# All gated rows of a mixer by seven block products, with ScalarE's deferrable work in a list of tasks

## The chip, the core and the metric

The kernel runs on one core of a Trainium2 chip. The metric is the device time of one execution in microseconds (us); the time before is the median of three runs. The engines named below are TensorE (PE in the profile; PEld is its weight load), VectorE (DVE), ScalarE (ACT), GpSimd (POOL) and SyncE (SP), which issues most of the loads.

## The reference

One step of an encoder trunk with two layers, for 640 tokens (512 of a prompt and 8 x 16 of running streams) with 1024 features, all in float32. Each layer is a feed-forward half-step, a mixer, and another feed-forward half-step. The change is in the mixer:

```
z = h @ w_in                      # conv B | conv C | conv V | q | k | v | gates
g_conv, g_attn = split(sigmoid(z_gates + b_gate))       # 1024 features each
y_conv = B * causal_conv3(C * V)                        # 512 features
y_attn = chunk-band attention, 8 heads of 64            # 512 features
m = g_conv * (y_conv @ w_conv_out) + g_attn * (y_attn @ w_attn_out)
x = x + m @ w_o
```

## The kernel before

**Numbers in two parts.** A float32 product is computed as three products of a faster 32-bit format: each operand is split into a high half (a cast on ScalarE) and a low half (source minus high half, on VectorE), and TensorE does hi x hi, hi x lo and lo x hi. So every weight needs one cast and one subtraction before it can be used.

**Weights.** The weights come as slabs of 128 x 1024, in the order of use, through three buffers (`raw`); their halves stand in three buffers each (`whi`, `wlo`). `prep` (line 351) casts the next slab on ScalarE and notes its low half; `flush` (line 367) issues the noted subtractions on VectorE; `source` (line 302) loads a slab and makes the sums of weight blocks. `slab` takes the next slab and prepares the one three places on; `quiet` only takes it; `ahead` makes the next slab's sums early.

**Seven products for eight.** Where two output rows of 128 features (or a row's two halves of the inner dimension) and two halves of the 640 tokens form a 2 x 2 block problem, the kernel uses the Winograd form of Strassen's scheme: seven block products instead of eight, with sums of weight blocks, sums of operand blocks ("mixing"), and sums of results. The seven are called by their operands: 11, 21, N6, T5, T7, 22, T4. Operands N6, T5, T7 and T4 are mixed, the other three are parts of the operand itself. A block product is 12 matmuls of 128 x 128 by 320 columns here. Such a group takes four weight slabs, the first three for two products each and the last for one. Each of seven products takes sums of weight blocks made on VectorE (one of them, in groups late enough, is summed by an accumulating DMA on GpSimd's queue, `lend_one`).

**The output stage** (`outputs`, line 1497) comes last in a mixer. It computes 16 gate rows of 128 features (0 to 7 for the conv branch, 8 to 15 for the attention branch) in pairs by `gate_pair` (the first pair is done earlier), and 8 output rows of each branch, which are multiplied by their gates and added up into `mm`. In it the instructions of TensorE, VectorE and ScalarE keep the order in which the program issues them, so each of these engines works through its own list, and an instruction that waits holds up all those behind it on its engine.

- `gate_pair(m)`: the products in the order 11, 21, N6, T5, T7, 22, T4. Product 11 goes into an accumulator `pa`; ScalarE copies it out (`c1`, capsm in the profile); then N6 adds to the same accumulator and is copied out (`u2`), and T7 and T4 add to it too. T5 goes into `pc`, is copied out (`c5`), and 22 adds to it. VectorE forms the rows u and g from these. u needs one more product with `rr` at the end, and a sigmoid on ScalarE comes after.
- `out(m)`: one row of a branch as a plain product over four blocks of the inner dimension, followed by the gating on VectorE.
- `rows`: four rows of a branch as one group of seven products, each into two 320-column parts, with the gating in between.

Before, rows 0 to 3 of each branch are plain (`out`), and rows 4 to 7 are a `rows` group. A sigmoid of u and g is kept in `lates` and issued by `due()` behind the copy of the next group's first product. The mixed operands of the conv branch are made step by step (`mixed`) between the plain rows and pair 4, those of the attention branch between pairs 8 and 14.

**Order of work before:** pair 2, four conv rows, pairs 4 and 6, conv rows 4 to 7, pair 8, two attention rows, pair 10, two attention rows, pairs 12 and 14, attention rows 4 to 7, and then the eight rows of the product with w_o.

Of the kernel before, what the change touches and what calls it, by code (L numbers as in the profile page):

```python
# [114 lines left out]
def mixer_order():  # L115

    mix = lambda *rows: ("mix", rows)
    out = [("v", None)] + [mix(("q", p), ("k", p)) for p in range(AW // P)]  # L120
    for c in range(0, CT, 2):
        out += [mix(("C", c + i), ("V", c + i)) for i in range(2)] + [mix(("B", c), ("B", c + 1))]
    gates = [mix(("g", m), ("g", m + 1)) for m in range(0, 2 * KT, 2)]
    out += gates[:2] + [("co", m) for m in range(4)] + gates[2:4] + [("rows", ("co", (4, 5, 6, 7)))]
    for i in range(2):
        out += [gates[4 + i], ("ao", 2 * i), ("ao", 2 * i + 1)]
    out += gates[6:] + [("rows", ("ao", (4, 5, 6, 7)))]
    return out + [("o", m) for m in range(KT)]
# [68 lines left out]
def trunk(ctx: ExitStack, tc: tile.TileContext, xin, wst, small, pbias, samplebias, kcache, vcache, gfin,  # L197
# [153 lines left out]
    def prep(i):  # L351
# [8 lines left out]
        o = 0  # L360
        for src, c in parts:
            d = slice(o, o + c.stop - c.start)
            o = d.stop
            ACT.copy(hi[:, d], src[:, c])  # L364
            pending.append((lo[:, d], src[:, c], hi[:, d]))

    def flush():
        for lo, src, hi in pending:
            DVE.tensor_tensor(out=lo, in0=src, in1=hi.bitcast(F32), op=ALU.subtract)  # L369
        pending.clear()  # L370
# [3 lines left out]
    def slab(hold=False):  # L374
# [10 lines left out]
        return ready[i], slabs[i]  # L385

# [1110 lines left out]
    def outputs(l, gp, X, st, cs, ycp, yas, sigmoid, gates):  # L1497
# [4 lines left out]
        ycs = [z[:, i] for z in ycp for i in range(2)]  # L1502
        mm = [spare[i // 2][:, i % 2] for i in range(CT)] + ycs
# [7 lines left out]
        lates = []  # L1511

        def due():
            for f in lates:
                f()
            lates.clear()

        def gate_pair(m, at):
            n = f"{l}_{m}"
            pa, pb, pc = (att(f"q{i}{n}")[:, :HT] for i in "abc")  # L1520
            s0 = quiet()
            block(pa, s0, 0, X11, every, True, True)
            ACT.copy(c1, pa)
            due()
            u, g = gates[m], gates[m + 1] = tmp(f"g{n}"), tmp(f"g{n}_1")
# [10 lines left out]
            ACT.copy(c5, pc)  # L1536
            at[1]()
            s2 = slab(True)[0]
# [5 lines left out]
            at[2]()  # L1544
            block(pc, s2, 1, X22, every, False, True)
            add(u[:, t2], pc, u2)
            s3 = slab(True)[0]
            DVE.tensor_tensor(out=u, in0=u, in1=rr, op=ALU.mult)
            lates.append(lambda: sigmoid(u, m))
            if m == 2:  # L1550
                for i in range(2):
                    sigmoid(gates[i], i)
            block(pa, s3, 0, XT4, every, False, True)
            DVE.tensor_tensor(out=g[:, t1], in0=pa, in1=rr[:, t1], op=ALU.mult)
            lates.append(lambda: sigmoid(g, m + 1, -1.0))
            flush()

        def parts(pool, tag, name, src):
            hi, lo = (pool.tile([P, T], F32R, tag=f"{tag}{i}", name=f"{name}{i}") for i in ("hi", "lo"))
            split(hi, lo, src)  # L1560
            return hi, lo

        def out(m, y, then=None, post=None):

            due()
            py = acc(f"py{l}_{m}")
            product(py, y)
            if then:
                then()
            g = gates[m]  # L1570
            if m < KT:
                DVE.tensor_tensor(out=halves(mm[m]), in0=two(py), in1=halves(g), op=ALU.mult)
            else:
                DVE.tensor_tensor(out=halves(g), in0=two(py), in1=halves(g), op=ALU.mult)
                add(mm[m - KT], mm[m - KT], g)
            flush()
            if post:
                post()

        yc, ya = [], []  # L1580
        mo = [None] * KT
        srcs = [yas[:, c, :] for c in range(CT)]
        x, moves = {}, []

        def take(y, name, cs, srcs):
            for c in cs:
                y.append(parts(gp, f"y{c}", f"{name}{l}_{c}", srcs[c]))

        def take_even(c):
            y = tuple(gp.tile([P, T], F32R, tag=f"y{c}{i}", name=f"ya{l}_{c}{i}") for i in ("hi", "lo"))  # L1590
            split(*(z[:, t1] for z in y), srcs[c][:, t1])
            ya.append(y)

        def low(lo, z, hi):
            DVE.tensor_tensor(out=lo, in0=z, in1=hi.bitcast(F32), op=ALU.subtract)

        def room(name):
            for k in EXTRA:
                x[name, k] = tuple(gp.tile([P, 2, HT], F32R, tag=f"x{EXTRA.index(k)}{i}",
                                           name=f"x{i}{name}{l}_{EXTRA.index(k)}") for i in ("hi", "lo"))  # L1600

        def minus(out, a):
            DVE.scalar_tensor_tensor(out=out, in0=a, scalar=-1.0, in1=out, op0=ALU.mult, op1=ALU.subtract)

        def mixed(i):

            z = ycp[i].rearrange("p c (a b) -> p (c a) b", a=2)
            e1, e2, o1, o2 = (z[:, k] for k in range(4))
            add(e1, e1, e2, ALU.subtract)
            add(e2, o2, e2, ALU.subtract)  # L1610
            minus(o2, e1)
            minus(o1, o2)
            yield
            for k in EXTRA:
                ACT.copy(x["co", k][0][:, i], z[:, 1 + EXTRA.index(k)])
            yield
            for k in EXTRA:
                hi, lo = (u[:, i] for u in x["co", k])
                low(lo, z[:, 1 + EXTRA.index(k)], hi)
            yield  # L1620
            hi, lo = (u[:, t2] for u in yc[2 * i])
            ACT.copy(hi, e1)
            yield
            low(lo, e1, hi)
            yield

        za = yas.rearrange("p (i c) (a b) -> p i (c a) b", i=2, a=2)

        def mix(n):

            e1, e2, o1, o2 = (za[:, :, k] for k in range(4))
            if n == 0:
                add(e1, e1, e2, ALU.subtract)
            elif n == 1:
                add(e2, o2, e2, ALU.subtract)
            else:
                minus(*((o2, e1) if n == 2 else (o1, o2)))

        def place(k):
            if k == XT5:  # L1640
                return [(*(u[:, t2] for u in ya[2 * i]), za[:, i, 0]) for i in range(2)]
            return [(*x["ao", k], za[:, :, 1 + EXTRA.index(k)])]

        def high(*ks):
            for k in ks:
                for hi, _, z in place(k):
                    ACT.copy(hi, z)

        def rest(*ks):
            for k in ks:  # L1650
                for hi, lo, z in place(k):
                    low(lo, z, hi)

        EXTRA = XT7, XT4, XN6

        def kind(name, i, k):
            if k in EXTRA:
                return tuple(z[:, i] for z in x[name, k])
            hi, lo = (yc if name == "co" else ya)[2 * i + (k in (X21, X22))]
            return tuple(z[:, t2 if k in (X22, XT5) else t1] for z in (hi, lo))  # L1660

        def rows(name, ms, first, mid=None, late=None, end=False, defer=False):

            n = f"{name}{l}_{ms[0]}"
            gs = [gates[m + (KT if name == "ao" else 0)] for m in ms]
# [3 lines left out]
            s1, s2, s5 = stage  # L1669

            def mul(ps, s, half, k, start):
                for u in range(2):
                    for i in range(2):
                        kp = half * NP + 2 * u + i
                        wh, wl = (z[:, kp * P : (kp + 1) * P] for z in s)
                        xh, xl = kind(name, i, k)
# [13 lines left out]
            def moved(r):  # L1690
                for u in range(2):
                    ACT.copy(mm[ms[2 * r + u]], gs[2 * r + u])

            w = quiet()
            mul(a, w, 0, X11, True)
            ACT.copy(s1, two(A))
            due()
            prep(used[0] + 1)
            flush()
            if first:  # L1700
                first()
            mul(b, w, 1, X21, True)
            add(s1, two(B), s1)
            w = slab(True)[0]
            flush()
            mul(a, w, 0, XN6, False)
            ACT.copy(s2, two(A))
            gated(0, [s1[:, u] for u in range(2)], t1)
            if mid:
                mid()  # L1710
            mul(c, w, 1, XT5, True)
            for u in range(2):
                ACT.copy(s5[:, u], c[u])
            w = slab(True)[0]
            mul(a, w, 0, XT7, False)
# [3 lines left out]
            if defer:  # L1719
                moves.append(lambda: gated(1, [s5[:, u] for u in range(2)], t2, -1.0))  # L1720
            else:
                gated(1, [s5[:, u] for u in range(2)], t2, -1.0)
            if late:
                late()
# [6 lines left out]
            if not end:  # L1731
                flush()
# [4 lines left out]
            if end:  # L1737
                flush()
# [700 lines left out]
```

## Time and profile before

| what | value |
|---|---|
| median of 3 runs | 2482.29 us (2481.04 to 2482.38) |
| span of the profiled execution, the time that the profile gives of it | 2479.9 us |
| median less that span | 2.4 us |
| granted TensorE clock, mean | 1.000 |
| TensorE busy | 2466.4 us, 99% |
| VectorE busy | 2182.6 us, 88% |
| ScalarE busy | 1386.7 us, 56% |
| output stage of layer 0 in the trace | from about 635 to 774 us |
| output stage of layer 1 in the trace | from about 1864 to 2003 us |

The span is counted from the first to the last instruction. A row of the timeline gives the start and the duration in us, the engine, the line of the kernel, the operation, output and inputs by their names in the program, and in brackets how long the engine was idle before and what ended that. A row of a grouped view gives the count, the busy time in us, the mean duration in ns, and the idle time before. A matmul's duration overlaps with the next one's, so TensorE's pace is read from the distance of the starts.

### The profile page before, as it was taken

How to read it: one execution, taken by the hardware profiler on the slowest of the kernel's cores; microseconds unless marked ns; L12 is line 12 of the kernel's file. 1: busy time of each engine (PE TensorE's matmuls, PEld its weight loads, DVE VectorE, ACT ScalarE, POOL GpSimd, SP SyncE). 2: the span in 40 equal slices, each digit the busy share in tenths (PEclk: the TensorE clock that was granted, in tenths of full speed). 3: DMA queues.
4: the chain of work that ended last, by engine and by line, in shares of the span. 5: the costliest groups of instructions: out<-in, count | busy, mean ns of one | idle time of the engine just before them, and what ended most of it. 6: DMA issues, size and time to landing. Idle time of an engine off the chain costs nothing.

```text
span 2479.9 us, 44056 instructions
## 1 busy us (share of the span) xinstructions
PE 2466.4 (99%) x17264; PEld 2414.6 (97%) x17264; DVE 2182.6 (88%) x3644; ACT 1386.7 (56%) x2231; POOL 320.8 (13%) x483
## 2 busy tenths in 40 slices
PE   9999999999999999999999999999999999999999
PEld 8999999889999999999999999998899999999998
DVE  7999998888888899998799999988888889999997
ACT  6555555665555555555665555566655556555555
POOL 0211112211000001111001010121110000111111
PEclk9999999999999999999999999999999999999999
DMA  4443444335344234444334343452453432444444
GB/s 155 128 120 101 124 117 120 114 110 175 102 118 123 93 102 107 112 118 119 109 94 109 110 117 102 117 128 102 138 167 94 119 119 92 108 113 107 112 117 117
DMA packets 113520, 288.16 MB, mean 116 GB/s; under 512 B 12992, under 2 KB 52544, under 8 KB 113312
## 3 DMA queue, kind: packets, MB, share of 16 engines
q1 hardware_dynamic: 69552, 220.10, 27.0%
q0 software_dynamic: 43328, 64.99, 13.8%
q8 instruction: 135, 2.21, 0.4%
q14 instruction: 73, 0.60, 0.1%
q10 hardware_dynamic: 432, 0.25, 0.0%
HBM read 239.48 MB, written 7.94 MB: 100 GB/s over the span
## 4 chain that ended last, share of the span: by engine, by line
PE 91%; DVE 4%; issue 3%; ACT 1%; DMA 1%; DVEq 0%; SPq 0%; ACTq 0%; POOLq 0%
PE pab L459 12%; PE paa L459 10%; PE pcb L459 6%; PE daa L1147 5%; PE dab L1147 5%; PE pca L459 5%; PE po L435 5%; PE qa L459 4%; PE pbb L459 3%; PE dca L1147 3%; PE dcb L1147 2%; PE pba L459 2%; PE ma_cv L459 2%; PE ma_qk L459 2%; PE py L435 2%
## 5 line engine op out<-in xcount | busy, mean ns | idle before, releaser
L364 ACT CAST whi<-raw 128x1024 fp32r<-128x1024 f32 (+1 forms) x578 | 502.3, 874 | 373.4 <-PE pbb L459 46.3
L369 DVE TENSOR_TENSOR wlo<-raw,whi 128x1024 fp32r<-128x1024 f32 (+1 forms) x578 | 577.0, 1001 | 135.4 <-ACT whi L364 131.2
L364 ACT CAST whi<-s 128x1024 fp32r<-128x1024 f32 (+1 forms) x162 | 152.9, 944 | 319.4 <-DVE s L296 113.5
L459 PE MATMUL pab<-xhib,whi 128*128 128x320 f32 x704 | 217.7, 309 | 0.0
L459 PE MATMUL pab<-xhib,wlo 128*128 128x320 f32 x704 | 217.2, 309 | 0.0
L459 PE MATMUL pab<-xlob,whi 128*128 128x320 f32 x704 | 217.2, 309 | 0.0
L459 PE MATMUL paa<-xhia,whi 128*128 128x320 f32 x640 | 197.8, 309 | 0.2 <-DVE ga L296 0.2
L459 PE MATMUL paa<-xhia,wlo 128*128 128x320 f32 x640 | 197.5, 309 | 0.0
L459 PE MATMUL paa<-xloa,whi 128*128 128x320 f32 x640 | 197.5, 309 | 0.0
L369 DVE TENSOR_TENSOR wlo<-s,whi 128x1024 fp32r<-128x1024 f32 (+1 forms) x162 | 176.3, 1088 | 4.0 <-ACT whi L364 4.0
L1169 POOL DMA_DIRECT2D x<-c_a x80 | 69.9, 1021 | 575.9 <-ACT ahia L1051 205.5
L1169 POOL DMA_DIRECT2D x<-c_b x72 | 63.2, 1014 | 583.1 <-ACT ahib L1051 205.4
L459 PEld LDWEIGHTS pab<-xhib,whi 128*128 128x128 f32 x704 | 132.1, 188 | 0.9 <-issue 0.9
L459 PEld LDWEIGHTS pab<-xhib,wlo 128*128 128x128 f32 x704 | 132.1, 188 | 0.0
L459 PEld LDWEIGHTS pab<-xlob,whi 128*128 128x128 f32 x704 | 132.1, 188 | 0.0
L459 PEld LDWEIGHTS paa<-xhia,whi 128*128 128x128 f32 x640 | 120.1, 188 | 1.1 <-DVE ga L296 0.4
L459 PEld LDWEIGHTS paa<-xloa,whi 128*128 128x128 f32 x640 | 120.1, 188 | 0.3 <-DVE xloa L703 0.3
L459 PEld LDWEIGHTS paa<-xhia,wlo 128*128 128x128 f32 x640 | 120.1, 188 | 0.1
L296 DVE TENSOR_TENSOR raw<-s,raw 128x512 f32<-128x512 f32 x162 | 110.7, 683 | 0.0
L459 PE MATMUL pcb<-xhib,wlo 128*128 128x320 f32 x352 | 108.8, 309 | 0.0
L459 PE MATMUL pcb<-xlob,whi 128*128 128x320 f32 x352 | 108.6, 309 | 0.0
L459 PE MATMUL pcb<-xhib,whi 128*128 128x320 f32 x352 | 108.6, 309 | 0.0
(909 smaller groups left out, 8201.3 us busy)
## 6 DMA issues: line engine op xcount, KB each, us to landing
raw<-in_wst SPq DMA_DIRECT2D x375, 512.0 KB, 3.5
x<-c_a POOLq DMA_DIRECT2D x80, 160.0 KB, 4.8
x<-c_b POOLq DMA_DIRECT2D x72, 160.0 KB, 4.2
lent<-in_wst POOLq DMA_DIRECT2D x36, 256.0 KB, 3.7
kc<-in_kcache SPq DMA_DIRECT2D x32, 256.0 KB, 4.8
vc<-in_vcache SPq DMA_DIRECT2D x16, 512.0 KB, 4.3
one<-in_wst POOLq DMA_DIRECT2D x32, 256.0 KB, 4.0
x<-u_a POOLq DMA_DIRECT2D x40, 160.0 KB, 4.1
```

Of the source, the lines that this page charges most:

```text
L296: DVE.tensor_tensor(out=out, in0=a, in1=b, op=op)
L364: ACT.copy(hi[:, d], src[:, c])
L369: DVE.tensor_tensor(out=lo, in0=src, in1=hi.bitcast(F32), op=ALU.subtract)
L435: PE.matmul(ps[:, a, :HT], w, x[a] if isinstance(x, tuple) else x[:, a * HT : (a + 1) * HT], start=first and j == 0 and not seeded, stop=l ...
L459: PE.matmul(ps, a, b, start=start and kp == 0 and j == 0, stop=stop and kp == NP - 1 and j == 2, skip_group_check=True)
L1147: PE.matmul(ps[u], w, y, start=start and i == 0 and j == 0, stop=i == 1 and j == 2, skip_group_check=True)
L1169: POOL.dma_start(x[ms[2 * u + r]][:, cols], z[:, u], accum_op=ALU.add)
```

## The change

**Rows.** All four groups of four rows become `rows` groups of seven products; `out` goes away. The order of the groups is now: pair 2, pair 4, conv rows 0 to 3, pair 6, conv rows 4 to 7, pairs 8 and 10, attention rows 0 to 3, pairs 12 and 14, attention rows 4 to 7. The order of the weights in memory follows.

**`rows`.** The products come in the order 11, T5, N6, 21, T7, 22, T4. All groups but the first of a layer copy product 11 from its accumulator into the second one, where 21 adds to it, instead of to a buffer and a sum on VectorE. In the conv groups three of the four gatings (six VectorE instructions) are put off to the next gate pair, where `due` issues them behind its second weight slab.

**Gate pairs.** u times `rr` moves from the place before product T4 to the place behind it and behind the low halves of the slab. Ahead of a `rows` group the next slab's second half is cast first, and its low half is issued before g's last product. Gates 2, 3, 6 and 7 are written where the gated rows will stand, so only rows 0, 1, 4 and 5 are moved by a copy.

**Tasks.** Sigmoids, the moves of gated rows and an early load of ScalarE's function table stand in one list, `tasks`, first in, first out. The places s (ahead of the first product), a, b, c and d (between later products) in `gate_pair` and `rows` call for one or two of them. At place s this comes ahead of ScalarE's copy of product 11.

**Mixed operands.** A class `Mixed` holds the parts of a branch's operand and issues the mixing on VectorE, the casts on ScalarE and the low halves on VectorE in steps over two gate pairs and the `rows` group behind them: for the conv branch pairs 2 and 4, for the attention branch pairs 8 and 10. A part is cast one place behind its mixing. The totals of rows 0 to 3 are formed in pair 12.

```diff
-        def gate_pair(m, at):
+        tasks = [lambda: ACT.activation(early, epst, AF.Sigmoid), lambda: sigmoid(gates[0], 0),
+                 lambda: sigmoid(gates[1], 1)]
+        def some(n=1):
+            def run():
+                for f in tasks[:n]:
+                    f()
+                del tasks[:n]
+            return run
+        def gate_pair(m, at={}, rows_next=False):
...
             s0 = quiet()
+            call("s")
             block(pa, s0, 0, X11, every, True, True)
             ACT.copy(c1, pa)
-            due()
-            prep(used[0] + 1)
+            following()
             flush()
-            at[0]()
             block(pb, s0, 1, X21, every, True, True)
             add(u[:, t1], pb, c1)
-            s1 = slab(True)[0]
+            s1 = quiet()
+            following()
             flush()
+            call("a")
             block(pa, s1, 0, XN6, every, False, True)
             ACT.copy(u2, pa)
+            call("b")
             block(pc, s1, 1, XT5, every, True, True)
             ACT.copy(c5, pc)
-            at[1]()
+            call("c")
...
             add(u[:, t2], pc, u2)
-            s3 = slab(True)[0]
-            DVE.tensor_tensor(out=u, in0=u, in1=rr, op=ALU.mult)
-            lates.append(lambda: sigmoid(u, m))
+            s3 = quiet()
+            following(rows_next)
+            if rows_next:
+                flush(1)
             block(pa, s3, 0, XT4, every, False, True)
             DVE.tensor_tensor(out=g[:, t1], in0=pa, in1=rr[:, t1], op=ALU.mult)
-            lates.append(lambda: sigmoid(g, m + 1, -1.0))
             flush()
+            DVE.tensor_tensor(out=u, in0=u, in1=rr, op=ALU.mult)
+            tasks.extend((lambda: sigmoid(u, m), lambda: sigmoid(g, m + 1, -1.0)))
+            call("d")
...
+                one = {"s": lambda: (hi(0, "11"), hi(1, "11"), hi(0, "2")),
+                       "a": lambda: (five(), lo(0, "11"), lo(1, "11"), lo(0, "2")),
+                       "b": lambda: (hi(0, "T5"), hi(1, "T5"), lo(0, "T5"), lo(1, "T5"), mix(0, "N6")),
+                       "d": lambda: hi(0, "N6")}
+                two = {"s": lambda: hi(1, "2"),
+                       "a": lambda: (lo(0, "N6"), lo(1, "2"), mix(1, "N6"), mix(0, "T7", "T4")),
+                       "b": lambda: (hi(1, "N6"), hi(0, "T"), mix(1, "T7", "T4"), lo(1, "N6")),
+                       "c": lambda: hi(1, "T")}
+                three = {"a": lambda: (lo(0, "T"), lo(1, "T"))}
...
             w = quiet()
-            mul(a, w, 0, X11, True)
-            ACT.copy(s1, two(A))
-            due()
-            prep(used[0] + 1)
+            call("s")
+            mul(a, w, 0, "11", True)
+            ACT.copy(two(B) if seed else s1, two(A))
+            following()
             flush()
...
+        gate_pair(2, joined({"a": [some()]}, one, {"d": [some()]}))
+        gate_pair(4, joined(two_, {"s": [some()], "d": [some()]}), True)
+        rows(yc, (0, 1, 2, 3), joined({"s": [some()]}, three, {"c": [some()]}), off)
+        gate_pair(6, joined({"s": [some()], "a": [due, ya.begin], "c": [some(2)]}), True)
+        rows(yc, (4, 5, 6, 7), joined({"s": [some()], "b": [some()]}), off)
+        one, two_, three = ya.steps(True)
+        gate_pair(8, joined(one, {"a": [due], "c": [some()], "d": [some()]}))
+        gate_pair(10, joined(two_, {"s": [some()], "d": [some()]}), True)
+        rows(ya, (0, 1, 2, 3), joined({"s": [some()]}, three, {"c": [some()]}))
+        gate_pair(12, joined({"s": [lambda: total(0)], "a": [lambda: total(1), some()],
+                              "b": [lambda: total(2, 3)], "c": [some()]}))
+        gate_pair(14, joined({"s": [some()], "a": [some()], "c": [lambda: (begun(*range(4)), given(0, 2))]}), True)
+        rows(ya, (4, 5, 6, 7), joined({"s": [some()], "a": [lambda: given(1, 3)], "c": [some()]}))
```

More of the change, by code (lines that the diff above doesn't have):

```diff
@@ L1580, in outputs @@
[L1580 to L1642, printed above, removed]
@@ L1666, in rows @@
+        seeded = [False]
+        def rows(y, ms, at={}, put_off=None):
+            n = f"{y.name}{l}_{ms[0]}"
+            co = y.name == "co"
+            gs = [gates[m + (0 if co else KT)] for m in ms]
             B, A = (acc(f"r{i}{n}") for i in "ba")
@@ L1669, in rows, with call @@
             s1, s2, s5 = stage
+            seed = seeded[0]
+            seeded[0] = True
+            def call(place):
+                for f in at.get(place, ()):
+                    f()
             def mul(ps, s, half, k, start):
@@ L1718, in rows @@
             ahead()
[L1719 to L1724, printed above, removed]
-            mul(c, w, 1, X22, False)
+            later(1, [s5[:, u] for u in range(2)], t2, -1.0)
+            mul(c, w, 1, "22", False)
             for u in range(2):
                 add(s2[:, u], c[u], s2[:, u])
-            w = slab(True)[0]
-            gated(0, [s2[:, u] for u in range(2)], t2)
-            mul(a, w, 0, XT4, False)
-            if not end:
-                flush()
-            gated(1, a, t1, -1.0)
-            if name == "co":
-                lates.append(lambda: moved(0))
-                moves.append(lambda: moved(1))
-            if end:
-                flush()
+            w = quiet()
+            following()
+            later(0, [s2[:, u] for u in range(2)], t2)
+            if co:
+                tasks.extend(lambda u=u: ACT.copy(mm[ms[u]], gs[u]) for u in range(2))
+            mul(a, w, 0, "T4", False)
+            flush()
+            later(1, a, t1, -1.0)
+        mo = [None] * KT
         def total(*ms):
@@ L1777, in outputs, with quarters, joined, due @@
-        rows("ao", (4, 5, 6, 7), None, lambda: given(1, 3), None, True)
+        def quarters(z):
+            return z.rearrange("p c (a b) -> p (c a) b", a=2)
+        def joined(*zs):
+            return {k: [f for z in zs for f in z.get(k, ())] for k in "sabcd"}
+        off = []
+        def due():
+            for f in off:
+                f()
+            off.clear()
+        each = {"s": [some()], "a": [some()]}
+        yc = Mixed("co", [quarters(z) for z in ycp])
+        ya = Mixed("ao", [quarters(yas[:, 2 * i : 2 * i + 2]) for i in range(2)])
@@ new lines, in outputs @@
+        one, two_, three = yc.steps()
+        gate_pair(2, joined({"a": [some()]}, one, {"d": [some()]}))
[5 more added lines that the diff above has]
+        gate_pair(8, joined(one, {"a": [due], "c": [some()], "d": [some()]}))
@@ L1778, in outputs @@
+        assert not tasks
         begun(*range(4, KT))
```

189 lines of the change are left out of this document (89 added, 100 removed).

## The prediction

> **What bounds the kernel now.** I read the first part of the page, then the busy times of the stretch that the change touches, then that stretch engine by engine in order of time.
>
> ```profile
> ## 1 busy us (share of the span) xinstructions
> PE 2466.4 (99%) x17264; PEld 2414.6 (97%) x17264; DVE 2182.6 (88%) x3644; ACT 1386.7 (56%) x2231; POOL 320.8 (13%) x483
> ```
>
> ```profile
> 634.90:774.30 139.40, 139.35 (x950) 139.05 (x950) 120.83 (x195) 80.00 (x133) 8.60 (x12) 1.00 0.36 106
> 677.20:689.50 12.30, 12.30 (x86) 12.30 (x85) 9.14 (x16) 6.32 (x12) 1.43 (x2) 1.00 0.44 129
> ```
>
> TensorE sets the time. The first row is the whole output stage of layer 0 (columns: stretch, length, then busy PE, PEld, DVE, ACT, POOL, granted clock, DMA share, GB/s). Its matmuls follow each other without a pause, and VectorE is busy 120.83 of 139.40 us. The second row is about one group of seven block products, 12.3 us, in the gate pairs: VectorE has 12.30 - 9.14 = 3.16 us to spare there.
>
> The only wait in that stage comes from VectorE, a late low half of a weight slab:
>
> ```profile
> L459 PEld LDWEIGHTS qa<-thi,wlo 128*128 128x128 f32 x84 | 15.8, 188 | 0.3 <-DVE wlo L369 0.3
> ```
>
> **What is removed: 48 matmuls.** First the counts of one layer, then two matmuls 48 apart on TensorE's timeline.
>
> ```profile
> L1678 PE MATMUL raco<-xhico,whi 128*128 128x320 f32 x12 | 3.7, 308 | 0.0
> ...
> L435 PE MATMUL py<-yc_0hi,whi 128*128 128x320 f32 x8 | 1.8, 308 | 0.0
> ```
>
> ```profile
> 682.50 0.31 PE L459 MATMUL qc<-hhim,whi 128*128 128x320 f32 x1
> ...
> 689.53 0.31 PE L1678 MATMUL raco<-xhico,whi 128*128 128x320 f32 x1
> ```
>
> Four plain rows of one branch are 8 x 3 combinations x 4 operands = 96 matmuls; a row group of seven products is 7 x 12 = 84 (the first row is one combination of three of its products). Each of two branches in each of two layers saves 12: 48. From 682.50 to 689.53 there are four products of 12, so a matmul costs 7.03 / 48 = 0.1465 us and a product 1.76 us. Gain: 48 x 0.1465 = **7.0 us**. The 0.3 us wait above, twice, lies at an order that goes away: 0.6 more.
>
> **What is added on VectorE.** The passage from gate pair 6 into the row group that follows it is the pattern for what comes; VectorE, then ScalarE, in order of time:
>
> ```profile
> 679.29 0.48 DVE L296 TENSOR_TENSOR g<-qb,capsm 128x320 f32<-128x320 f32 x1
> 679.69 0.68 DVE L369 TENSOR_TENSOR wlo<-raw,whi 128x512 fp32r<-128x512 f32 x1
> 682.77 0.49 DVE L296 TENSOR_TENSOR g<-qa,c 128x320 f32<-128x320 f32 x1 [2.39 <-PE qa L459]
> 683.29 0.49 DVE L1541 TENSOR_TENSOR g<-g,rrm 128x320 f32<-128x320 f32 x1
> 683.70 1.22 DVE L369 TENSOR_TENSOR wlo<-raw,whi 128x1024 fp32r<-128x1024 f32 x1
> 684.84 0.68 DVE L296 TENSOR_TENSOR raw<-raw 128x512 f32<-128x512 f32 x1
> 685.56 0.69 DVE L296 TENSOR_TENSOR s<-raw,raw 128x512 f32<-128x512 f32 x1
> 686.17 0.48 DVE L296 TENSOR_TENSOR g<-qc,capsm 128x320 f32<-128x320 f32 x1
> 686.68 0.83 DVE L1548 TENSOR_TENSOR g<-g,rrm 128x640 f32<-128x640 f32 x1
> 687.43 0.48 DVE L1554 TENSOR_TENSOR g<-qa,rrm 128x320 f32<-128x320 f32 x1
> 687.83 0.68 DVE L369 TENSOR_TENSOR wlo<-s,whi 128x512 fp32r<-128x512 f32 x1
> 688.43 0.68 DVE L369 TENSOR_TENSOR wlo<-raw,whi 128x512 fp32r<-128x512 f32 x1
> ```
>
> ```profile
> 680.94 0.43 ACT L1536 COPY c<-qc 128x320 f32<-128x320 f32 x1 [1.33 <-PE qc L459]
> 681.26 1.05 ACT L364 CAST whi<-raw 128x1024 fp32r<-128x1024 f32 x1
> 686.36 0.62 ACT L364 CAST whi<-s 128x512 fp32r<-128x512 f32 x1 [4.05 <-DVE s L296]
> 686.89 0.62 ACT L364 CAST whi<-raw 128x512 fp32r<-128x512 f32 x1
> 688.01 0.70 ACT L1696 COPY capsm<-raco 128x640 f32<-128x640 f32 x1 [0.51 <-ACT whi L364]
> 688.60 1.55 ACT L1354 ACTIVATE g<-g,sm 128x640 f32<-128x640 f32 x2
> ```
>
> Back to back, VectorE's starts are 0.40 us apart for 320 elements (0.51 where the next needs the result), 0.60 for 512, 0.75 for 640 and 1.14 for 1024. The mixing and its low halves have the same prices:
>
> ```profile
> L1595 DVE TENSOR_TENSOR xloco<-yc,xhico 128x320 fp32r<-128x320 f32 x6 | 2.6, 484 | 0.0
> L1595 DVE TENSOR_TENSOR xloao<-ya,xhiao 128x640 fp32r<-128x640 f32 x3 | 2.4, 818 | 0.0
> L1603 DVE SCALAR_TENSOR_TENSOR yc<-yc 128x320 f32<-128x320 f32 x4 | 2.0, 493 | 0.1
> ```
>
> A row group costs VectorE 6.1 us for its weights (one low half of 1024, five of 512, three sums) and 4.7 for eight gatings, the sum of s5 and two of s2. Per layer the change adds two groups less one s1 sum (20.9), the mixed operands (10.7 of low halves, 6.6 of mixing) and four totals (3.0), 41 in all; it removes eight low halves of y (6.0), the gating of eight plain rows (9.0), four low halves of plain slabs (4.6) and the old mixing and its low halves (12.4), 32. So VectorE goes from 121 to 130 us while TensorE goes from 139.4 to 135.6: still less, but only by 4%, and unevenly.
>
> **Where it lands on the path: a sigmoid ahead of an evacuation.** In a gate pair the new order on VectorE is: u's sum, (one low half where rows follow), g's T4 product, the remaining low halves, and only then u times rr. That pair's sigmoid of u is the first task of the next group in five places a layer (into rows co 4, pair 10, rows ao 0, pair 14, rows ao 4: I followed the list of tasks through the eleven groups), and it stands ahead of ScalarE's copy of the first product. Behind that copy waits the third product, which adds to the same accumulator; everything else of ScalarE is queued there too. In the old order the copy (688.01) went ahead of the sigmoids (688.60).
>
> Reordering the rows above: u's sum 686.17, low half 686.57, g 687.17, low half 687.57, u times rr 688.17 to 689.00. The sigmoid follows at 689.03 and leaves ScalarE after 0.72 (two take 1.55, one 0.83), so the copy of 640 runs 689.75 to 690.45. The third product was to start at 689.53: **0.95 us late**. Into a gate pair the copy is 0.43 instead of 0.70: **0.68 late**. This chain starts at VectorE's 682.77, which waited for TensorE, so spare time earlier does not shorten it. Three of 0.95 and two of 0.68: **4.2 us a layer**. In the seeded groups the copy of 640 goes from accumulator to accumulator, which no row shows; bounds are 0.70 (688.01, out of the accumulator) and 0.71 (into it):
>
> ```profile
> L429 ACT ACTIVATE pdb<-x 128x640 f32<-128x640 f32 x7 | 5.0, 710 | 0.9 <-DVE x L1174 0.7
> ```
>
> **Two casts ahead of the copy of c5** (pairs 4 and 10). After the low half that starts at 679.69 VectorE is free at 680.29. Now it has there a low half of 320 and one of 640, the mixing of N6, T7 and T4: T4 is done at 680.29 + 0.40 + 0.75 + 3 x 0.40 + 0.1 = 682.74. ScalarE's cast of T (0.73) waits for it and stands ahead of the copy of c5, which then ends near 683.8 instead of 681.37; product 22, due at 682.50 into the accumulator that it empties, starts 1.3 late. Bounds: 0.5, if VectorE comes to these steps early, and 2.0, if it is already behind. I take 1.3: **2.6 a layer**.
>
> **Pair 2 into pair 4:** between the casts (done near 687.4) and the copy of c1 ScalarE gets a cast of 320, a sigmoid, a cast of 640 and a sigmoid: 0.36 + 0.72 + 0.63 + 0.72, and the copy ends at 690.2 instead of before 689.53: **0.7**, between 0 and 1.0.
>
> **VectorE overrun.** Pair 8 gets six deferred gatings (2.4) and 2.8 of low halves and mixing against 3.16 spare: 2.0 over. The T7 sum is then late and the T4 product waits: 0.9 taken, between 0 and 2.0. Pair 10 adds 3.7, 0.5 over; the row groups come to 12.3 of 12.3 with their low halves; pair 12 has 3.0 of totals right ahead of its T7 sum. So the four later sigmoids start from a VectorE that is behind. A stall gives back its own length; I take 0.6 at each, 2.4, between 0 and 1.5 each.
>
> Per layer 4.2 + 2.6 + 0.7 + 0.9 + 2.4 = 10.8, twice 21.6. Less 7.6: **+14.0 us**. On the profiled span of 2479.9 us that is 2493.9; the median of the runs, 2482.29, lies 2.4 above the span, so **2496.3**.
>
> **At no cost.** The two extra lent halves and the slabs that are held longer: a load lands in 3.5 us, and the slab freed late is wanted some 12 us later; the DMA share is 0.36 in the stage. Without that cover each new group could wait 3.5. ScalarE's new weight casts fit beside the 80.00 of 139.40 that it is busy. Table load and the moves of gated rows change place, not number.
>
> ```profile
> raw<-in_wst SPq DMA_DIRECT2D x375, 512.0 KB, 3.5
> ```
>
> **Rivals.** *VectorE keeps up, not slower* (0.08). If ScalarE's waits end 0.95 us earlier, all terms above vanish together: 2482.3 - 7.6 = 2474.7. For it: VectorE's total stays under TensorE's. Against: the chain from 682.77 needs 6.2 us of VectorE in series. It decides at the point where the sigmoid leaves ScalarE before the first product ends. *Only the five sigmoids bind* (0.09): 8.4 - 7.6, 2483.1; it needs the casts to be in time and no overrun. *ScalarE's order is not the program's*, so that the change does not do what it says: the rows of ScalarE stand in program order, and I give this nothing of its own beyond the first rival. *The clock drops at the stalls* (0.02). At the kernel's start, after 5.56 us without work, matmuls start 0.26 apart, not 0.146:
>
> ```profile
> 6.00 0.47 PE L435 MATMUL poa<-x2hia,whi 128*128 128x320 f32 x1
> 6.26 0.47 PE L435 MATMUL poa<-xloa,whi 128*128 128x320 f32 x1
> ```
>
> If each of some 18 stalls were followed by 12 such matmuls, that is 18 x 12 x 0.12 = 26 more, 2522. The Trainium skill (TensorE: Matmul & The Clock Gate, "A second HAM failure mode: psum-queue depth-cycling") says that short idles between matmul groups can make the clock swing; its Part 1 asks for a whole idle window of about 3.4 us, and by that nothing is added. The stalls forecast here are 0.7 to 1.6 us; no run here shows which of the two holds for them.
>
> **How the numbers follow.** The forecast has 0.81. Its own range goes from 5.6 a layer (the casts at 0.5 each, 0.4 for the rest) to 15 (the four later sigmoids at 1.0, the rest at their upper bounds): 2486 to 2505. The low end takes in the five-sigmoid rival: 2483. Faster or slower by 0.2% is 5.0 us, about what a measurement of this kernel can tell. Faster: 0.08. Same: the 0.09 and a small part of the forecast, 0.11. Slower: 0.81.
>
> **What would show it.** Right: TensorE waits of 0.7 to 1.7 us on ScalarE's copies (of the first product and of c5), idle time of ScalarE ahead of sigmoids that ends with VectorE's u times rr, and VectorE over 90% busy in the stage. Wrong: an output stage of 135.6 us without gaps; low halves of weights (not copies) as the releasers; waits on raw slabs; or a clock below 1.00.

## The result: 0.7% slower, and the profile after

The changed kernel takes 2498.68 us (median of 4 runs, 2498.05 to 2499.56) against 2482.14 (4 runs, 2481.04 to 2482.38): a ratio of 1.0069, with a 95% interval of 1.0054 to 1.0083. That is 16.5 us more. The forecast was 2496.3, 14.0 more, between 2483 and 2505. The profiled span is 2497.4 us, 17.5 more than before.

The first part of the page (busy time of each engine, share of the span, instructions), after:

```profile
PE 2463.8 (99%) x17216; PEld 2407.4 (96%) x17216; DVE 2199.4 (88%) x3704; ACT 1397.9 (56%) x2263; POOL 326.4 (13%) x491
```

TensorE has 48 matmuls less, 17216 instead of 17264. The share of busy time shows nothing of the loss. The output stage of layer 0, by stretches (length, busy PE, PEld, DVE, ACT, POOL, clock, DMA share, GB/s), does:

```profile
634.90:783.80 148.90, 138.65 (x929) 135.92 (x928) 130.39 (x227) 84.60 (x146) 11.46 (x16) 1.00 0.37 107
```

It was 139.4 us with TensorE busy throughout; now it is 148.9, with some 10 us in which TensorE works on nothing. Layer 1 is longer by about the same. The waits of TensorE name the places (engine and line, what it waited for, us in total over both layers, times, longest):

```profile
PE qa L462 <- ACT capsm L1536: 8.2, 6, 1.8
...
PE raao L1668 <- ACT rbao L1689: 5.0, 4, 1.5
PE qc L462 <- ACT c L1550: 3.4, 4, 0.9
PE raco L1668 <- ACT rbco L1689: 1.6, 2, 0.8
PE qa L462 <- DVE g L294: 1.3, 2, 0.6
```

None of these was there before. L1536 and L1689 are ScalarE's copies of the first product (of a gate pair and of a row group), L1550 is the copy of c5, and g at L294 is pair 8's T7 sum. Together 18 waits of 19.5 us.

**A fresh sigmoid ahead of a copy.** Into attention rows 0 to 3, layer 0, in order of time: VectorE, ScalarE, TensorE.

```profile
730.46 0.48 DVE L1566 TENSOR_TENSOR g<-qa,rrm 128x320 f32<-128x320 f32 x1
730.86 0.68 DVE L368 TENSOR_TENSOR wlo<-s,whi 128x512 fp32r<-128x512 f32 x1
731.46 0.82 DVE L1568 TENSOR_TENSOR g<-g,rrm 128x640 f32<-128x640 f32 x1
```

```profile
732.31 0.83 ACT L1357 ACTIVATE g<-g,sm 128x640 f32<-128x640 f32 x1 [1.39 <-DVE g L1568]
733.05 0.68 ACT L1689 COPY rbao<-raao 128x640 f32<-128x640 f32 x1
```

```profile
732.43 0.31 PE L1668 MATMUL rcao<-y4ao_1hi,wlo 128*128 128x320 f32 x1
733.78 0.42 PE L1668 MATMUL raao<-y4ao_0hi,whi 128*128 128x320 f32 x1 [1.04 <-ACT rbao L1689]
734.03 0.31 PE L1668 MATMUL raao<-y4ao_0lo,whi 128*128 128x320 f32 x1
734.18 0.31 PE L1668 MATMUL raao<-y4ao_0hi,wlo 128*128 128x320 f32 x1
```

u times rr (L1568) ends at 732.28, ScalarE has stood idle for 1.39 us with that sigmoid at its head, and the copy behind the sigmoid lets the third product go at 733.78. The last three rows also give the price of a wait: the starts are 1.35 and then 0.25 apart, where 0.1465 is the pace, so this one costs 1.20 + 0.10 = 1.30 us, though the column says 1.04. All prices below are taken from such distances.

**Casts ahead of the copy of c5**, pair 4, layer 0:

```profile
656.66 2.10 DVE L1617 SCALAR_TENSOR_TENSOR yc<-yc 128x320 f32<-128x320 f32 x5
```

```profile
657.19 0.46 ACT L1603 CAST y4co_1hi<-yc 128x320 fp32r<-128x320 f32 x1 [2.00 <-DVE yc L1617]
657.99 0.72 ACT L1603 CAST y4co_0hi<-yc 128x640 fp32r<-128x640 f32 x1 [0.34 <-DVE yc L1617]
658.62 0.42 ACT L1550 COPY c<-qc 128x320 f32<-128x320 f32 x1
```

Each cast waits for its mixing, the copy waits behind both casts, and product 22 starts at 659.10.

**A list with no gap in it.** Into pair 10 ScalarE, once it has begun, works without a pause; it has too much ahead of the copy:

```profile
715.12 0.62 ACT L363 CAST whi<-s 128x512 fp32r<-128x512 f32 x1 [4.19 <-DVE s L294]
715.65 0.61 ACT L363 CAST whi<-raw 128x512 fp32r<-128x512 f32 x1
716.17 0.46 ACT L1603 CAST y4ao_0hi<-ya 128x320 fp32r<-128x320 f32 x1
716.53 0.72 ACT L1721 COPY yc<-g 128x640 f32<-128x640 f32 x1
717.16 0.72 ACT L1603 CAST y2ao_1hi<-ya 128x640 fp32r<-128x640 f32 x1
717.84 0.83 ACT L1357 ACTIVATE g<-g,sm 128x640 f32<-128x640 f32 x1
718.57 0.41 ACT L1536 COPY capsm<-qa 128x320 f32<-128x320 f32 x1
```

The list also begins late. Its first cast waits for VectorE's sum of the slab (the 4.19 us in brackets) and starts 2.34 us before the third product is due (717.46, one pace behind the matmul at 717.31). In pairs 6, 8 and 12 of the same layer, where the first copy holds up nothing, that cast starts 3.06 to 3.44 us before. By this reckoning, some 0.7 to 1.1 us of the 1.68 lost here is VectorE's lateness, and the rest is the list. It is the same into pair 4: there the cast starts 2.43 us before in layer 0 and 2.88 in layer 1, which is the difference between 1.61 and 1.17 in the table.

Each place against its forecast (us for one layer; measured: layer 0 / layer 1, from the distances of TensorE's starts):

| what is late | forecast | measured |
|---|---|---|
| copy, conv rows 4 to 7 | 0.95 | 1.06 / 1.06 |
| copy of c1, pair 10 | 0.68 + 0.6 | 1.68 / 1.67 |
| copy, attention rows 0 to 3 | 0.95 + 0.6 | 1.32 / 1.32 |
| copy of c1, pair 14 | 0.68 + 0.6 | 2.04 / 1.64 |
| copy, attention rows 4 to 7 | 0.95 + 0.6 | 1.73 / 1.72 |
| copy of c5, pairs 4 and 10 | 2.6 | 2.24 / 2.24 |
| copy of c1, pair 4 | 0.7 | 1.61 / 1.17 |
| T7 sum, pair 8 | 0.9 | 0.90 / 0.90 |
| copy of u2, pair 12 | 0 | 0.34 / 0.33 |
| sum | 10.8 | 12.9 / 12.1 |

25.0 in both layers, less the forecast's 7.6 for what goes away, is 17.4; the span grew by 17.5. In pair 12 it is ScalarE's copy of u2 that is late (L1547): it ends at 749.90, just ahead of the T7 product at 749.95.

```profile
748.43 1.14 ACT L363 CAST whi<-raw 128x512 fp32r<-128x512 f32 x2 [2.84 <-DVE raw L294]
749.48 0.42 ACT L1547 COPY capsm<-qa 128x320 f32<-128x320 f32 x1
```

### The profile page after: what moved, and what is told of

It is laid out like the page before. It is cut to its first block, busy times and chain, and to the rows that moved or that the text cites. A ratio compares the mean times of both kernels' runs of the same rounds, so it can differ in the third digit from the quotient of the medians.

```text
span 2497.4 us, 44084 instructions
## 1 busy us (share of the span) xinstructions
PE 2463.8 (99%) x17216; PEld 2407.4 (96%) x17216; DVE 2199.4 (88%) x3704; ACT 1397.9 (56%) x2263; POOL 326.4 (13%) x491
## 4 chain that ended last, share of the span: by engine, by line
PE 84%; DVE 9%; ACT 3%; DMA 2%; issue 2%; SPq 0%; DVEq 0%; ACTq 0%; POOLq 0%
PE pab L462 12%; PE paa L462 11%; PE pcb L462 6%; PE daa L1150 5%; PE pca L462 5%; PE dab L1150 5%; PE po L438 5%; PE pbb L462 3%; DVE wlo L368 3%; PE dca L1150 3%; PE pba L462 3%; PE dcb L1150 2%; PE ma_cv L462 2%; PE ma_qk L462 2%; PE pv L1831 2%
## 5 line engine op out<-in xcount | busy, mean ns | idle before, releaser
L294 DVE TENSOR_TENSOR raw<-s,raw 128x512 f32<-128x512 f32 x166 | 113.4, 683 | 0.0
```

The source lines that it names most:

```text
L294: DVE.tensor_tensor(out=out, in0=a, in1=b, op=op)
```

## The experiments

Two theories were put against each other. **O**: each wait is made by the order, by what the program writes ahead of a copy on ScalarE's list or ahead of a sum on VectorE's. **V**: VectorE has too much work in these groups, and moving steps only moves the wait. Each experiment was timed beside the kernel before, whose median was 2480.86 us for experiments 1 to 4, 2481.52 for 5 to 8 and 2480.96 for 9, against 2482.14 in the comparison above. So what an experiment brings back is read from its distance to its own kernel before, beside the 16.5 us of the changed kernel. The intervals of the ratios are 2 to 4 us to either side: gains under that, in experiments 3, 4 and 7, are not shown by the times, and what those three show is read from the waits in their traces.

In the diffs, `s` to `d` are the places for deferred work; `t` (right behind the copy of product 11) and `f` (behind the next slab's preparation) are new.

**1. The first task behind the first copy**

```diff
             ACT.copy(c1, pa)
+            call("t")
...
             ACT.copy(two(B) if seed else s1, two(A))
+            call("t")
...
-        gate_pair(4, joined(two_, {"s": [some()], "d": [some()]}), True)
+        gate_pair(4, joined(two_, {"t": [some()], "d": [some()]}), True)
```

(and so in the other seven groups that call for a task at `s`)

> The changed kernel, with the first task of every group issued behind ScalarE's copy of product 11 and not ahead of it; nothing else moves. Theory O (the order on ScalarE makes the waits): the five waits on that copy go from 1.06 to 1.85 us each to 0.2 or less, the one of pair 4 loses one sigmoid (0.72); per layer 1.06 + 1.68 + 1.32 + 1.85 + 1.73 + 0.72 = 8.4, so 16 to 17 us off 2498.7: about 2482. The waits on c5 (1.1) and of pair 8 (0.9) stay. Theory V (VectorE has too much work in the stage, and the place of the sigmoid only decides where that shows): VectorE's work and order are the same, so the waits come back at late low halves of weights, and the time stays within 3 us of 2498.7.

Measured: 2488.52 us, 1.0032 (1.0020 to 1.0043) of the kernel before. The waits for the first copies of all three row groups are gone, but others grew:

```profile
PE qc L462 <- ACT c L1551: 6.3, 4, 1.6
...
PE qa L462 <- ACT capsm L1536: 2.3, 4, 0.6
...
PE raao L1669 <- ACT rs L1701: 1.0, 2, 0.5
```

The copy of c5 now costs 1.85 instead of 1.12 each time, and the second copies (L1701) of attention rows 4 to 7 are late. It is 7.7 us above its kernel before, so 8.9 of 16.5 us came back, neither O's whole nor V's nothing: the sigmoid is out of the first copy's way and stands in the way of what follows.

**2. u times rr ahead of the last block product again**

```diff
             if rows_next:
                 flush(1)
+            DVE.tensor_tensor(out=u, in0=u, in1=rr, op=ALU.mult)
             block(pa, s3, 0, XT4, every, False, True)
...
             flush()
-            DVE.tensor_tensor(out=u, in0=u, in1=rr, op=ALU.mult)
```

> The changed kernel, with u times rr issued on VectorE ahead of product T4 again; the sigmoid stays ahead of the copy. O: the sigmoid no longer waits for the whole tail of VectorE's list; the chain ends 1.3 us earlier (g's last product, one or two low halves), so the five waits fall to 0.4 or less: 11 to 15 us off, 2484 to 2488. V: the same work in another order on VectorE, nothing gained: 2497 to 2500.

Measured: 2489.17 us, 1.0032 (1.0020 to 1.0045): just above O's range and far from V's. VectorE does the same work, and 8.2 us came back because one 0.82 us instruction stands two or three instructions earlier. In layer 0 the wait at conv rows 4 to 7 is gone (0.07), those of attention rows 0 to 3 and 4 to 7 fell to 0.33 and 0.73 and that of pair 14 to 0.40. But pair 10 keeps 1.62 of 1.68 and pair 4 has 1.71 for 1.61: there it was not u times rr that held up the copy.

**3. The casts of N6 and T behind the copy of c5**

```diff
-                       "b": lambda: (hi(1, "N6"), hi(0, "T"), mix(1, "T7", "T4"), lo(1, "N6")),
-                       "c": lambda: hi(1, "T")}
+                       "b": lambda: mix(1, "T7", "T4"),
+                       "c": lambda: (hi(1, "N6"), hi(0, "T"), lo(1, "N6"), hi(1, "T"))}
```

> The changed kernel, with the casts of N6 and T of the mixed operands issued behind the copy of c5 in pairs 4 and 10. O: the two waits of 1.12 us at product 22 go, four in all: 2494 to 2495; the five waits at the first copy stay. V: 2497 or more, the wait moves to the next release from VectorE.

Measured: 2497.42 us, 1.0069 (1.0054 to 1.0084), the ratio of the changed kernel, and V's reading of this step. The waits on c5 are gone, and new ones stand a product or two later:

```profile
PE raao L1668 <- ACT rbao L1689: 5.8, 4, 1.5
...
PE rcao L1668 <- DVE wlo L368: 0.6, 2, 0.3
PE rcco L1668 <- DVE wlo L368: 0.6, 2, 0.3
```

The low halves of the weights are late for the rows' second product (0.56 each), and attention rows 0 to 3 wait 1.73 instead of 1.32. The waits on c5 had cost 4.5 us in both layers; moving the steps from one crowded place to the next brought nothing that the times show.

This profile, taken of the longest of four runs (2500.78 us, the others 2496.9 to 2497.5), shows one thing more. Behind the wait into pair 14 of layer 0 TensorE slowed down:

```profile
761.04 0.41 PE L462 MATMUL qa<-thi,whi 128*128 128x320 f32 x1 [1.80 <-ACT capsm L1536]
...
762.11 0.47 PE L462 MATMUL qa<-thi,whi 128*128 128x320 f32 x1
762.38 0.47 PE L462 MATMUL qa<-tlo,whi 128*128 128x320 f32 x1
```

From 761.87 to 765.31 the granted clock is 0.50 and the matmuls start 0.265 us apart, which costs 1.5 us. No other of the eleven profiles has such a stretch behind a wait.

**4. Conv rows 4 to 7 gated in their own group**

```diff
-        rows(yc, (4, 5, 6, 7), joined({"s": [some()], "b": [some()]}), off)
+        rows(yc, (4, 5, 6, 7), joined({"s": [some()], "b": [some()]}))
```

> The changed kernel, with the gating of conv rows 4 to 7 done in its own group, so that pair 8 loses 2.4 us of VectorE's work. O: the wait of pair 8 (0.9) goes and the later ones lose up to 0.5 each, at most 4 us in all: 2494.5 to 2497; the wait ahead of conv rows 4 to 7 stays at about 1.06. V: pair 8 is where the overrun starts, so the four waits that follow it (1.3 to 1.9 each) go as well: 10 us or more, 2489 or less.

Measured: 2496.29 us, 1.0061 (1.0046 to 1.0076). Pair 8's wait fell from 0.90 to 0.11, pair 10's grew in layer 0 to 1.99 (a slab landed 0.22 us late there) and stayed in layer 1, and the others stay about the same. So the six gatings that had been put off to pair 8 made its wait, as O had it.

**5. Both orders of the sigmoid (1 and 2 together)**

> Only the two orders of the fresh sigmoid are undone, both at once: first task behind the first copy, and u x rr ahead of the last block product. Each alone gave 2489. If both repair the same waits (theory O: a sigmoid that waits for u x rr in front of the copy is one wait with two parts), 2487 us (2486 to 2489), with waits of about 1.8 us for the copy of c5 in pairs 4 and 10. If they repair different waits, the gains add, 2479 us.

Measured: 2487.53 us, 1.0023 (1.0014 to 1.0032). 8.9 and 8.2 do not add: together they bring 10.5. It is one wait with two parts, and 1.83 at each copy of c5 is left.

**6. All four edits**

> The four edits together: first task behind the first copy, u x rr ahead of the last block product, the casts of N6 and T behind the copy of c5, rows 4 to 7 of the conv gated in their own group. Without any of its new waits the changed kernel would take about 2498.7 - 2 x 12.75 = 2473.2 us. Theory O (each wait is set by what the program writes ahead of it on one engine): some 6 us a layer are left, in pairs 4 and 10 and in the rows' second product, 2485 us (2483 to 2487). Theory V (VectorE has too much work in these groups, and moving operations only moves the wait): no better than the best single edit, 2488 us or more.

Measured: 2483.47 us, 1.0009 (1.0000 to 1.0018). A little better than O's 2485, and level with the kernel before. Pair 10 (0.91), the T4 products of pairs 4 and 10 (0.6 each), the low halves for the rows' second product (0.57 each) and smaller ones in pairs 4, 12 and 14 and in attention rows 4 to 7 are left.

**7. VectorE's load taken away: no mixing of T7 and T4**

```diff
-                    else:
+                    elif k == "N6":
                         out, a = {"N6": (o2, e2), "T4": (o1, o2), "T7": (e1, o2)}[k]
```

> The changed kernel with the mixings of T7 and T4 left out (eight VectorE operations of 128x320 a layer; the products T7 and T4 then work on unmixed operands, so part of the computation is changed), everything else in its place. Theory O: only the two waits for the copy of c5 fall, from 1.1 to about 0.6 us, since half of each is the casts that stand ahead of the copy on ScalarE; 2496 us (2495 to 2497.5). Theory V: the lateness of VectorE in pairs 4 and 10 and behind them goes with its work: c5 waits near nothing, rows ao0 and pair 12 with shorter waits, 2493 us or less.

Measured: 2496.64 us, 1.0062 (1.0048 to 1.0076): O's number. With eight VectorE steps fewer in a layer, only the waits on c5 fell:

```profile
PE raao L1668 <- ACT rbao L1689: 5.0, 4, 1.5
PE qc L462 <- ACT c L1550: 1.7, 4, 0.4
PE raco L1668 <- ACT rbco L1689: 1.6, 2, 0.8
PE qa L462 <- DVE g L294: 1.3, 2, 0.6
```

Those on c5 went from 3.4 to 1.7: by idle time half of each was VectorE's mixing, and half is left with the two casts ahead of the copy. The copies of the row groups wait as long as with the mixing (5.0 and 1.6). Those of the gate pairs have 7.9 for 8.2; the difference is a late slab in the changed kernel's pair 14, which comes below.

**8. The same steps, spread over more places**

No step is left out; the mixing of the conv operand starts a product or two earlier, the attention's first operand is cast in the rows ahead of pair 8, the last casts stand in the rows that use them, totals stand one to a place. The list takes over u times rr ahead of T4 (experiment 2) and the gating of conv rows 4 to 7 in their own group (experiment 4), and in three groups of rows the first task behind the first copy (experiment 1). Two groups of the eleven, from before and after:

```diff
-        rows(yc, (4, 5, 6, 7), joined({"s": [some()], "b": [some()]}), off)
+        at = {
+            "t": [lambda: (some()(),)],
+            "b": [lambda: (ya.mix(0, "T5"),)],
+            "c": [lambda: (some()(), ya.high(0, "11"), ya.low(0, "11"),)],
+        }
+        rows(yc, (4, 5, 6, 7), at)
...
-        gate_pair(12, joined({"s": [lambda: total(0)], "a": [lambda: total(1), some()],
-                              "b": [lambda: total(2, 3)], "c": [some()]}))
+        at = {
+            "f": [lambda: (total(0),)],
+            "a": [lambda: (total(1), some()(),)],
+            "b": [lambda: (total(2),)],
+            "c": [lambda: (some()(),)],
+        }
+        gate_pair(12, at)
```

> The same operations as in the changed kernel, none left out, but their places chosen so that no copy of a product has more than one deferrable operation ahead of it: the conv's mixing begins a product or two earlier in pair 2, the attention's first operands already in the rows ahead of pair 8, the last casts only in the rows that use them, totals and half splits of pairs 12 and 14 one place apart, u x rr ahead of the last product. VectorE and ScalarE do as much work as before the edit. Theory O: waits of 1 to 2.5 us a layer are left, 2475 to 2478 us, which is faster than the kernel before (2482) by 4 to 7. Theory V: the work is the same, so the waits come up elsewhere, 2485 us or more.

Measured: 2478.02 us, 0.9985 (0.9976 to 0.9994): at the upper end of O's range, and a little faster than the kernel before. The list does not keep to one step ahead of a copy everywhere, as the expectation has it: pair 2 has four casts at `s`, pair 4 three steps of ScalarE ahead of the copy of c5, pair 10 two steps at `s`. What was left in layer 0, by the waits of TensorE in that stretch:

```profile
PE qa L462 <- ACT capsm L1549: 1.3, 1, 1.3
PE qa L462 <- ACT capsm L1536: 0.4, 1, 0.4
```

The 1.3 is new, in pair 2. ScalarE's timeline there:

```profile
639.63 1.57 ACT L363 CAST whi<-raw 128x1024 fp32r<-128x1024 f32 x2 [1.92 <-DVE raw L294]
641.22 1.28 ACT L1513 ACT_TABLE_LOAD   x1
...
642.62 0.41 ACT L1549 COPY capsm<-qa 128x320 f32<-128x320 f32 x1
```

Mixing and low halves stood ahead of a weight slab's sum on VectorE; ScalarE stood idle for 1.92 us for that sum, and the slab's casts, the load of the function table and the copy of u2 came late after it.

**9. The places chosen a second time**

```diff
-            "t": [lambda: (yc.mix(0, "T5"), yc.mix(1, "T5"), yc.low(1, "2"), yc.mix(1, "N6"),)],
...
+            "c": [lambda: (yc.low(1, "2"),)],
...
-            "s": [lambda: (some()(), ya.high(1, "2"),)],
+            "s": [lambda: (some()(), ya.low(1, "2"),)],
```

(the lines with a minus are those of experiment 8; the first change is in pair 2, the second in pair 10; the mixings of T5 stand at `s`, behind the casts, that of N6 for the second half in pair 4, and the cast of 2 for pair 10 in pair 8)

> The list of places chosen a second time. The first list (2478.0 us) had put three VectorE steps ahead of a weight slab's sum in pair 2, and a wait of 1.4 us had come up there; here they stand behind it, the casts of 640 elements for N6, T7 and T4 are one to a place, and one ScalarE step stands ahead of the first copy of pair 10 instead of two. Same operations, same number. Theory O (the place decides): pair 2 and pair 10 lose their waits, 0.5 to 1.5 us a layer are left, 2475 to 2477 us. Theory V (VectorE's sum of work decides): about 2 us a layer stay wherever the steps are put, 2478 us.

Measured: 2474.51 us (2474.07 to 2475.37, 10 runs) against 2480.96 (14 runs): 0.9974 (0.9965 to 0.9984), a little under O's range. The first part of its page, and its output stage:

```profile
PE 2459.4 (99%) x17216; PEld 2407.1 (97%) x17216; DVE 2198.4 (89%) x3704; ACT 1397.4 (57%) x2263; POOL 325.6 (13%) x491
```

```profile
634.90:770.60 135.70, 135.70 (x924) 135.08 (x923) 128.60 (x224) 84.11 (x146) 11.42 (x16) 1.00 0.41 117
```

The counts are those of the changed kernel, 3704 on VectorE and 2263 on ScalarE. The stage has no wait of TensorE left, with VectorE busy for 128.60 of 135.70 us, 95%. V falls: the work fits. What cost time were orders in which steps of VectorE or ScalarE that were late, or too long together, stood ahead of what TensorE needed next.

## Why the prediction was right

**The gain was right.** 48 matmuls at 0.1465 us plus 0.6 are 7.6 us, and without the stalls the time was to be 2474.7. Experiment 9 is that kernel in effect: 2474.51. That the two agree so closely is partly luck, as the kernel before was at 2480.96 in that comparison: the gain is 6.5 us there, with an interval of 4.0 to 8.7, and 7.3 by the two profiled spans (2479.9 and 2472.6). Its output stage in layer 0, from the first matmul at 634.62 to the first of the product with w_o at 770.66, takes 136.0 us, where the prediction named 135.6 without gaps.

**VectorE's load was right.** From 121 to 130 us in the stage was forecast; the rows say 120.83 and 130.39, and over the whole run VectorE's busy time grew by 16.8 us, 8.4 a layer. But the sign "over 90% busy" was wrong, 88%: the stalls lengthened the stage too. 95% appears once they are gone.

**The five first copies.** The mechanism, a sigmoid waiting for u times rr ahead of a copy, holds in four of five places: experiment 2 takes away all or most of the wait there by moving one instruction. Conv rows 4 to 7 came at 1.06 for 0.95. In the fifth, pair 10, the step failed: following the list of tasks was right, but u times rr was not what held up the copy, and issuing it earlier brought 0.06 us. ScalarE's row of a cast, a move, a cast and a sigmoid, 2.4 us without a gap, behind weight casts that VectorE had made late, was in the way, as at pair 4. The forecast had priced such a list only at pair 4, and too low, 0.7 for 1.61 and 1.17, because it let the weight casts there be in time. That 0.68 + 0.6 for pair 10 comes near to the measured 1.68 is luck as far as the 0.68 goes.

**VectorE's lateness** (0.6 at each of four sites) was the term with the least behind it. With pair 10 set aside, what stood over 0.95 or 0.68 at the other three in layer 1 was 0.37, 0.96 and 0.77, 0.7 on average. In pair 12 the prediction had three totals ahead of the T7 sum and gave them no price. They cost none: the T7 sum (752.90 to 753.38) was done ahead of the T4 product at 753.58. The 0.34 there is another wait: the first total (746.98) and the end of the gating of the attention rows stood ahead of a slab's sum on VectorE (747.71), ScalarE's casts of that slab waited 2.84 us for it, and the copy of u2 stood behind them. In layer 0 pair 14 took 0.4 more; there a slab landed late, the one wait on a transfer that TensorE, VectorE or ScalarE show in the stage:

```profile
755.35 0.69 DVE L294 TENSOR_TENSOR raw<-raw 128x512 f32<-128x512 f32 x1 [0.30 <-DMA raw<-in_wst]
```

So "at no cost" for the loads holds but for this.

**Copy of c5** (1.3 each for 1.12) and **pair 8** (0.9 for 0.90) hold, each with its cause shown, by experiments 3 and 7 and by experiment 4. That pair 8 came out to the hundredth is luck: 0.9 was picked between 0 and 2.0.

**The sum** was 3.5 us short by the spans (17.5 for 14.0), 2.5 by the medians (16.5): 1.3 to 2.1 a layer, mostly the long lists into pairs 4 and 10, the first copy of pair 14 and the unpriced pair 12.

**The rivals.** *VectorE keeps up* gave 2474.7 for an order in which ScalarE is in time; that is the price of the order, and experiment 9 shows it, but it was not the order that the change has. *Only the five bind* (2483.1) falls: c5, pair 4 and pair 8 cost 4.3 to 4.8 a layer. *The clock drops*: the granted clock was 1.00 in the stage, and behind each wait one matmul stood 0.25 from the next and the pace was 0.15 again. The swing of the Trainium skill's "A second HAM failure mode: psum-queue depth-cycling" (TensorE: Matmul & The Clock Gate), which would have been 26 us more, did not show in the changed kernel. The Trainium skill (TensorE: Matmul & The Clock Gate, Part 1) wants a whole idle window of about 3.4 us for a drop, and 18 waits of up to 1.8 us in the changed kernel agree with it. Experiment 3 does not: there the clock fell to 0.50 behind a wait of 1.80 us, which cost 1.5 us. So the rival was wrong for the changed kernel's profile, but a single drop behind a wait shorter than 3.4 us does occur. Why it came there, and not behind the wait of 1.77 us at the same place in the changed kernel, stays open.

What also stays open: the prices of single steps are entangled. Experiments 1, 3 and 4 each took a wait away and lengthened another, so the table says where the time was lost, not what each place would give alone.

## What to carry to other kernels

Where an engine works through its list in order, a copy that frees an accumulator should have nothing ahead of it that can be late or long: ask of each deferrable step what it waits for, and how much of such work stands in a row. Moving a bunch of steps from one place to the next moves the wait with it; spread thinner, the same steps cost TensorE no wait here, with VectorE at 95%. And a busy share does not tell these cases apart: VectorE's share was lower in the kernel with the stalls.

## What was not expected of the hardware

A wait of TensorE cost about 0.26 us more than its idle time says. In the rows at 733.78 the idle time is counted from the end of a matmul that lasts 0.31 while the pace is 0.1465 (0.16 more), and the first matmul behind the wait stands 0.25 from the next (0.10 more). 18 waits with 19.5 us of idle time, 4.7 us for this and 0.7 for pair 12 make 24.9 of the table's 25.0 us; read from the waits alone, a fifth of the loss would have had no place. And in experiment 3 the granted clock fell to 0.50 for 3.44 us behind a wait of 1.80 us, the only such drop behind a wait in these profiles.
